# First attention half issued ahead of the convolution, and the second half's stacked queries and keys in a pool of their own

## The chip, the cores and the metric

The kernel runs on one core of a Trainium2 chip. The metric is the device time of one execution in microseconds (us); lower is better. The core has a tensor engine (PE) for matmuls and transposes, a vector engine (DVE), a scalar engine (ACT), a general engine (POOL), and a sync engine (SP) that here only issues transfers (DMAs). Each engine works through a queue of its own, strictly in order; an instruction that waits for another engine or for a transfer holds up all that stands behind it in its queue.

## The reference: what is computed

One layer of a decoder with D = 1024, for 1024 prompt tokens and 8 samples of 8 new tokens (T = 1088 rows together):

```
h    = rmsnorm(x);  proj = h @ w_in
o_rw = RWKV-7 time mixing(proj)             # 4 heads of 64
o_cv = cb * conv3(cc * cx)                  # short causal convolution, 256 channels
o_sb = stick_breaking(q, k, v)              # 8 heads of 64
x    = x + concat(o_rw, o_cv, o_sb) @ w_out
x    = x + square(relu(rmsnorm(x) @ w_up)) @ w_down
x    = x + sigmoid(rmsnorm(x) @ w_ple_gate) * (p @ w_ple_proj)
```

Stick-breaking attention, for a query at position i and keys j < i: z = q.k/8 + bias, and the weight of key j is sigmoid(z_j) times the product of (1 - sigmoid(z_m)) over all m with j < m < i. That product is a running product over the keys, taken from the last key backwards. The new sample tokens also attend to 512 cached keys, which lie in pages whose row numbers come from `page_table`.

## The kernel before

**Numbers.** Every matmul of weights is computed to fp32 accuracy as three matmuls of high and low parts (hi·hi, hi·lo, lo·hi): in lines 169 to 171 for the input projection, the convolution among it, and in lines 1093 to 1095 for the output projection and the MLP. The high part of a weight is a cast on ACT (`wh`, lines 158 and 1073), the low part a subtraction, mostly on POOL (`wl`, lines 159 and 1074).

**What sets the order.** The program writes the work in an order of emission, and a scheduler then fixes each engine's queue before the run: what was emitted earlier comes first where it can, and later work is put into the gaps that the scheduler's own estimate shows. `run(*gens)` (line 654) takes generators and advances them in turn, one step of each; so `run(*[conv]*5, *[att]*4)` emits five steps of the convolution for every four of the attention. Memory comes from pools on two sides of the on-chip memory; a tile of a pool waits for those who last used the memory under it (`reuse_waits="tile"`).

**The stretch in question.** After the RWKV part comes `wkv_sample_chunk`, then the convolution together with the first half of the attention (query rows 0 to 511), then part A (rows 0 to 511) of the output projection and the MLP, and beside it the second half of the attention (query rows 512 to 1023), and later the cached pages (`decode`) and part B.

- `convolution` (line 975): 18 pieces of 24 matmuls (432 in all), each piece evicted by ACT or DVE; three loads of weights of 1024 columns, each split by ACT (L158) and POOL (L159).
- `attention(ap, q0, q1, ...)` (line 875) has 16 units, 8 heads by two blocks of 256 queries. `prep(h)` loads for a head the stacked keys and queries (`stk_k`, `stk_q`, `stk_x`) and `vs`, on SP. `weights` takes two groups of 128 queries, each with L keys (128 to 512 in the first half, 640 to 1024 in the second). For each group: scores on PE in chunks of 512 columns (L913, L914); two sigmoids on ACT, `beta` (L915) and `keep` (L916); the mask on the last 128 columns on POOL, for `keep` and for `beta` (L920); the running product on DVE (L922); and `beta * keep` (L924) on DVE, for every other group of the second half on POOL. `values`, two units later, transposes the weights on PE (L942), splits them in `wth` (ACT) and `wtl` (DVE, L61), and multiplies with `vs` (L952, L953); ACT and DVE evict `o` (L955, L956), and SP stores it.
- Part A: `load_x` transposes the rows of x on PE (L1302). `load_mix` loads the mixed rows (`mixl`) and splits them in `mh` (ACT, L1289) and `ml` (DVE, L1290). `out_proj(A, 0, 4)` multiplies by the first half of `w_out` in 96 matmuls of 512 columns, 24 for each DVE eviction pair (L1395).
- `page_rows` loads the page table (`pti`) and computes row numbers `idx` on DVE (L1113, L1114); `row_constants` makes masks for the samples (POOL and DVE, L1131 to L1170); then POOL issues four fetches of cached pages with these row numbers (`kpg`, L1118).

The names `b`, `b_6783` and so on in rows are buffers of the accumulators (banks).

Of the kernel before, what the change touches and what calls it, by code (L numbers as in the profile page):

```python
# [21 lines left out]
F32 = mybir.dt.float32  # L22
F32R = mybir.dt.float32r
# [20 lines left out]
CA = (5, 4)  # L44
AB_ = 2
# [3 lines left out]
def hybrid_step(ctx: ExitStack, tc: tile.TileContext, I, O):  # L49
# [6 lines left out]
    def f(t):  # L56
        return t.bitcast(F32)
# [9 lines left out]
    def banks(*ids):  # L67

        turn = itertools.cycle(ids)

        def take():
            i = next(turn)
            return psum.tile([128, 512], F32, name=f"b{i}", bufs=1)

        return take
# [28 lines left out]
    km = tc.alloc_tile_pool(name="wkv_masks", bufs=1, side="right", reuse_waits="tile")  # L104
# [549 lines left out]
    def run(*gens):  # L654

        gens = list(gens)
        while gens:
            for g in list(gens):
                if next(g, gens) is gens:
                    gens.remove(g)  # L660
# [103 lines left out]
    kp = tc.alloc_tile_pool(name="wkv", bufs=1, side="right", reuse_waits="tile")  # L764
    wkv_prompt_chunks()
    kp.release()
    kp = tc.alloc_tile_pool(name="wkv_s", bufs=1, side="right", reuse_waits="tile")
    ap = tc.alloc_tile_pool(name="att_a", bufs=1, side="right", reuse_waits="tile")
# [103 lines left out]

    def attention(ap, q0, q1, zbank, wbank, obank, AHEAD):

        bias = ap.tile([128, 2, 8], F32, name="bias")
        src = I["sb_bias"]
        SP.dma_start(bias[:, 0], bass.AP(tensor=src.tensor, offset=src.offset, ap=[[0, 128], [1, 8]]))
        V.tensor_scalar(bias[:, 1], bias[:, 0], -1.0, None, op0=ALU.mult)  # L880
# [3 lines left out]
        def prep(h):  # L884

            stk = []
            for name, n, r0 in (("k", 1, 0), ("q", 0, 256 * q0), ("x", 0, 256 * q0)):
                r = slice(r0, 256 * q1)
                o = ap.tile([128, 256 * q1 - r0], F32R, name=f"stk_{name}", bufs=2)
                if name == "x":  # L890
                    for e in range(2):
                        SP.dma_start(f(o)[64 * e:64 * e + 64], stk_s[n, h, 1 - e, :, r])
                else:
                    SP.dma_start(f(o), stk_s[n, h, :, :, r].rearrange("e d t -> (e d) t"))
                stk.append(o)
            vs = ap.tile([128, 2 * q1, 128], F32R, name="vs", bufs=2)
            SP.dma_start(f(vs), v_s[h, 0:2 * q1].rearrange("i p e -> p i e"))
            heads[h] = stk + [vs]
# [59 lines left out]

        units = [(h, qb) for h in range(8) for qb in range(q0, q1)]
        prep(0)  # L960
        for n in range(len(units) + AHEAD):
            if n < len(units):
# [72 lines left out]

    wkv_sample_chunk(banks(2))
    conv, att = convolution(), attention(ap, 0, 2, banks(3, 4), banks(5, 6), banks(7), AA)
    run(*[conv] * CA[0], *[att] * CA[1])
    cv.release()
    wpool.release()  # L1040
    hpool.release()
# [435 lines left out]
    w_out = I["w_out"][0]  # L1477

    A = Part(xpa, wka, hpa, 0, 512, ((0, 512),))
    A.load_x(acc)  # L1480
    A.load_mix(range(0, 4))
    out_proj(A, 0, 4)
    A.load_mix(range(4, 8))
    ap.release()
    kp.release()
    km.release()
    pre = tc.alloc_tile_pool(name="pages", bufs=1, side="right", reuse_waits="tile")
    page = page_rows(pre)
    db, neg, own, same = row_constants(pre)
    first = [page(pre, "kpg", krows, 0, n, 4) for n in range(PAGES)]  # L1490
    ap = tc.alloc_tile_pool(name="att_b", bufs=1, side="right", reuse_waits="tile")
    run(attention(ap, 2, 4, banks(3, 4), banks(5, 6), banks(7), AB_))
    ap.release()
    dp = tc.alloc_tile_pool(name="dec", bufs=1, side="right", reuse_waits="tile")
    decode()
    dp.release()
# [5 lines left out]
    B.load_x(tr)  # L1502
    out_proj(A, 4, 4)
    A.norm("g_mlp", acc, wide=True)
    u = up(A, 0)
# [111 lines left out]
```

## Time and profile before

| | |
|---|---|
| time of three runs, us | 1713.23, 1717.89, 1720.93; median 1717.89 |
| the profiled execution, us | 1714.63, with a span of 1712.9 |
| PE busy | 1645.4 us, 96% of the span; mean granted clock 0.983 |
| DVE, ACT, POOL busy | 1082.4, 792.7 and 704.4 us (63%, 46%, 41%) |
| chain of work that ended last | PE 79%, DVE 8%, DMA 5%, ACT 3% |

The profile gives the profiled execution alone; its time is 3.3 us below the median of the three runs. The granted clock is the share of TensorE's full clock that the chip allowed: 1.00 is 2.4 GHz, and a row at half of it is 1.2 GHz. In rows of a timeline the first number is the start in us from the start of the span, the second the busy time in us, and a bracket at the end gives the idle time ahead of the row on its engine and what ended it. A pitch is the distance between the starts of two rows.

### The profile page before, as it was taken

To read this page: it belongs to the slowest core of one execution; us is meant where nothing else is said; L and a number is where in the kernel's file an instruction comes from. 1 tells how busy PE (TensorE), PEld (TensorE's weight loads), DVE (VectorE), ACT (ScalarE), POOL (GpSimd) and SP (SyncE) were. 2 spreads that over 40 slices of the span, in tenths; PEclk is the share of its full clock that TensorE was granted. 3 is DMA by queue.
4 is the path that set the end of the run, shared out by engine and by line. 5 is a ranking of instruction groups with operands and counts; after the bars stand their busy time and mean duration, and the time that the engine had idled before them with its cause. 6 is when DMAs were issued, how large, how long until landed. Compare 5 with 4: busy or idle time off the path is not lost.

```text
span 1712.9 us, 30744 instructions
## 1 busy us (share of the span) xinstructions
PE 1645.4 (96%) x11901; PEld 1485.0 (87%) x11901; DVE 1082.4 (63%) x1830; ACT 792.7 (46%) x1563; POOL 704.4 (41%) x754
## 2 busy tenths in 40 slices
PE   6999999999899899999999999998899999999998
PEld 5898988889888777888887778977899999999898
DVE  6266844465276859878753345267877888778432
ACT  6633433333353657666544444463443444438321
POOL 4123221123332654443435544365755556538210
PEclk9999999999999899999999999999999999999999
DMA  6134466235523763443345556221322232222211
GB/s 189 52 116 132 144 165 170 69 89 152 154 76 115 217 180 104 129 127 102 91 132 172 166 160 210 90 74 50 111 88 86 90 96 87 87 84 77 82 46 41
DMA packets 207061, 197.03 MB, mean 115 GB/s; under 512 B 58113, under 2 KB 172449, under 8 KB 206786
## 3 DMA queue, kind: packets, MB, share of 16 engines
q1 hardware_dynamic: 197186, 174.08, 34.2%
q0 software_dynamic: 5120, 16.78, 3.3%
q10 hardware_dynamic: 4608, 4.20, 1.0%
q8 instruction: 94, 1.54, 0.4%
q14 instruction: 53, 0.43, 0.1%
HBM read 158.03 MB, written 36.98 MB: 114 GB/s over the span
## 4 chain that ended last, share of the span: by engine, by line
PE 79%; DVE 8%; DMA 5%; ACT 3%; issue 2%; SPq 1%; POOL 1%; ACTq 0%; POOLq 0%; DVEq 0%
PE b L1093 14%; PE b L1095 14%; PE b L1094 13%; PE b L1438 3%; PE b L1437 3%; PE b L1436 3%; PE b L169 3%; PE b L170 3%; PE b L171 3%; PE b L797 2%; PE b L795 2%; PE b L942 2%; PE b L796 2%; DVE keep L922 1%; DMA wr<-in_w_in 1%
## 5 line engine op out<-in xcount | busy, mean ns | idle before, releaser
L1074 POOL TENSOR_TENSOR wl<-wr,wh 128x512 fp32r<-128x512 f32 x172 | 237.9, 1393 | 249.2 <-ACT wh L1073 232.6
L1073 ACT CAST wh<-wr 128x512 fp32r<-128x512 f32 x292 | 179.3, 622 | 293.4 <-PE b L1094 207.0
L1093 PE MATMUL b<-ah,wh 128*128 128x288 f32 (+1 forms) x768 | 255.6, 333 | 6.4 <-DVE x L1475 3.5
L1475 DVE TENSOR_TENSOR x<-b,x 128x288 f32<-128x288 f32 (+1 forms) x384 | 199.1, 527 | 98.7 <-PE b L1095 97.5
L1094 PE MATMUL b<-al,wh 128*128 128x288 f32 (+1 forms) x768 | 252.5, 329 | 0.0
L1095 PE MATMUL b<-ah,wl 128*128 128x288 f32 (+1 forms) x768 | 252.3, 329 | 0.0
L1093 PE MATMUL b<-nh,wh 128*128 128x512 f32 (+1 forms) x448 | 165.8, 371 | 1.0 <-DVE x L1395 1.0
L1094 PE MATMUL b<-nl,wh 128*128 128x512 f32 (+1 forms) x448 | 164.9, 368 | 0.8 <-DVE nl L1317 0.8
L1095 PE MATMUL b<-nh,wl 128*128 128x512 f32 (+1 forms) x448 | 165.0, 368 | 0.0
L1093 PEld LDWEIGHTS b<-ah,wh 128*128 128x128 f32 x768 | 144.9, 189 | 18.7 <-DVE x L1475 6.1
L1095 PEld LDWEIGHTS b<-ah,wl 128*128 128x128 f32 x768 | 144.8, 189 | 10.4
L1094 PEld LDWEIGHTS b<-al,wh 128*128 128x128 f32 x768 | 144.9, 189 | 9.5 <-issue 0.8
L795 PE MATMUL b<-wh,h_hi 128*128 128x256 f32 x432 | 127.0, 294 | 5.1 <-ACT sq L805 5.1
L797 PE MATMUL b<-wh,h_lo 128*128 128x256 f32 x432 | 126.5, 293 | 0.0
L796 PE MATMUL b<-wl,h_hi 128*128 128x256 f32 x432 | 124.5, 288 | 0.0
L169 PE MATMUL b<-h_hi,wh 128*128 128x384 f32 (+1 forms) x336 | 114.3, 340 | 1.9 <-ACT xs L333 1.3
L159 POOL TENSOR_TENSOR wl<-wr,wh 128x1024 fp32r<-128x1024 f32 x26 | 64.8, 2507 | 121.4 <-ACT wh L158 121.3
L170 PE MATMUL b<-h_lo,wh 128*128 128x384 f32 (+1 forms) x336 | 113.2, 337 | 0.3 <-DVE h_lo L201 0.3
L171 PE MATMUL b<-h_hi,wl 128*128 128x384 f32 (+1 forms) x336 | 111.8, 333 | 0.0
L922 DVE TENSOR_TENSOR_SCAN keep<-keep,onesq 128x128 f32<-128x128 f32 (+3 forms) x64 | 97.6, 1525 | 21.1 <-POOL keep L920 17.9
L1074 DVE TENSOR_TENSOR wl<-wr,wh 128x512 fp32r<-128x512 f32 x120 | 100.2, 837 | 9.6 <-ACT wh L1073 7.9
L1074 POOL TENSOR_TENSOR wsl<-s,wsh 128x512 fp32r<-128x512 f32 x64 | 88.5, 1404 | 37.9 <-ACT wsh L1073 37.8
(425 smaller groups left out, 4312.9 us busy)
## 6 DMA issues: line engine op xcount, KB each, us to landing
wr<-in_w_up SPq DMA_DIRECT2D x64, 512.0 KB
wr<-in_w_down SPq DMA_DIRECT2D x64, 512.0 KB
wr<-in_w_in SPq DMA_DIRECT2D x26, 512.0 KB
wr<-in_w_out SPq DMA_DIRECT2D x16, 512.0 KB
xt<-in_x_prompt SPq DMA_DIRECT2D x8, 512.0 KB
stk_s<-sth ACTq DMA_DIRECT2D x32, 128.0 KB
stk_s<-stl SPq DMA_DIRECT2D x32, 128.0 KB
v_s<-spl SPq DMA_DIRECT2D x16, 256.0 KB
```

What stands on the lines that cost most here:

```text
L169: PE.matmul(ps[:, :n], wh[:, k, c], a, start=(k == 0), stop=False)
L170: PE.matmul(ps[:, :n], wh[:, k, c], b, start=False, stop=False)
L171: PE.matmul(ps[:, :n], wl[:, k, c], a, start=False, stop=(k == nk - 1))
L795: PE.matmul(o, a, w[0][:, k, :], start=(k == 0), stop=False)
L796: PE.matmul(o, a, w[1][:, k, :], start=False, stop=False)
L797: last = PE.matmul(o, b, w[0][:, k, :], start=False, stop=(k == 7))
L1073: S.copy(h3, src)
L1074: (sub or G).tensor_sub(l3, src, f(h3))
L1093: PE.matmul(ps[:, :n], w(0, k, m), a, start=(k == 0), stop=False)
L1094: PE.matmul(ps[:, :n], w(0, k, m), b, start=False, stop=False)
L1095: PE.matmul(ps[:, :n], w(1, k, m), a, start=False, stop=(k == nk - 1))
L1475: V.tensor_add(p.x[:, m, t0:t0 + n], ps[:, :n], p.x[:, m, t0:t0 + n])
```

## The change

The first half of the attention is now emitted whole, and the convolution after it. The second half's generator is made before part A's loads, and its first step (`next(steps)`) is taken there: it emits the bias, the loads of heads 0 and 1, and the scores and weights of the first unit. The rest of it (`run(steps)`) stands where the whole stood. Its `bias` and `stk_*` tiles are in a pool of their own (`stk_b`), and the pools of the earlier parts on that side are released ahead of part A's loads, for this and for the pool of the pages.

```diff
-    def attention(ap, q0, q1, zbank, wbank, obank, AHEAD):
-
-        bias = ap.tile([128, 2, 8], F32, name="bias")
+    def attention(ap, q0, q1, zbank, wbank, obank, AHEAD, sp=None):
+
+        sp = sp or ap
+        bias = sp.tile([128, 2, 8], F32, name="bias")
...
-                o = ap.tile([128, 256 * q1 - r0], F32R, name=f"stk_{name}", bufs=2)
+                o = sp.tile([128, 256 * q1 - r0], F32R, name=f"stk_{name}", bufs=2)
...
     conv, att = convolution(), attention(ap, 0, 2, banks(3, 4), banks(5, 6), banks(7), AA)
-    run(*[conv] * CA[0], *[att] * CA[1])
+    run(att)
+    run(conv)
...
     A = Part(xpa, wka, hpa, 0, 512, ((0, 512),))
+    ap.release()
+    kp.release()
+    km.release()
+    pre = tc.alloc_tile_pool(name="pages", bufs=1, side="right", reuse_waits="tile")
+
+    sp = tc.alloc_tile_pool(name="stk_b", bufs=1, side="right", reuse_waits="tile")
+    ap = tc.alloc_tile_pool(name="att_b", bufs=1, side="right", reuse_waits="tile")
+    steps = attention(ap, 2, 4, banks(3, 4), banks(5, 6), banks(7), AB_, sp)
+    next(steps)
     A.load_x(acc)
     A.load_mix(range(0, 4))
     out_proj(A, 0, 4)
     A.load_mix(range(4, 8))
-    ap.release()
-    kp.release()
-    km.release()
-    pre = tc.alloc_tile_pool(name="pages", bufs=1, side="right", reuse_waits="tile")
     page = page_rows(pre)
     db, neg, own, same = row_constants(pre)
     first = [page(pre, "kpg", krows, 0, n, 4) for n in range(PAGES)]
-    ap = tc.alloc_tile_pool(name="att_b", bufs=1, side="right", reuse_waits="tile")
-    run(attention(ap, 2, 4, banks(3, 4), banks(5, 6), banks(7), AB_))
+    run(steps)
     ap.release()
+    sp.release()
```

Line numbers of the changed program are one higher from line 877 on, two higher from line 1040 on.

Three places of the scheduled queues follow, as text, without times.

PE where the attention's first scores stand. Before, 120 of the convolution's 432 matmuls stand ahead of the first score (L913); `L512` is a matmul of the RWKV sample chunk:

```order
L171 MATMUL b_5459<-h_hi_81,wl 128x384
L913 MATMUL b_5509<-stk_k,stk_q 128x128
L914 MATMUL b_5509<-stk_k,stk_x 128x128
L913 MATMUL b_5523<-stk_k,stk_q 128x256
L914 MATMUL b_5523<-stk_k,stk_x 128x256
L169 MATMUL b_5678<-h_hi_80,wh 128x320
```

Of the change, where 11 matmuls of the convolution stand ahead of it:

```order
L170 MATMUL b_6285<-h_lo_82,wh 128x384
L914 MATMUL b_5365<-stk_k,stk_q 128x128
L914 MATMUL b_5379<-stk_k,stk_q 128x256
L171 MATMUL b_6285<-h_hi_80,wl 128x384
L169 MATMUL b_6285<-h_hi_81,wh 128x384
L170 MATMUL b_6285<-h_lo_83,wh 128x384
L171 MATMUL b_6285<-h_hi_81,wl 128x384
L915 MATMUL b_5365<-stk_k,stk_x 128x128
```

The scores moved forward by about a hundred of the convolution's matmuls, and the convolution goes on behind them.

PE from the convolution's last matmul on. Before, the first half's scores (of 128 and 256 keys) and values are still under way there:

```order
L171 MATMUL b_6509<-h_hi_81,wl 128x320
L913 MATMUL b_6550<-stk_k,stk_q 128x128
L914 MATMUL b_6550<-stk_k,stk_x 128x128
L757 MATMUL b_5320<-ident,GS 64x64 x16
L952 MATMUL b_6423<-wth,vs 128x256
L953 MATMUL b_6423<-wtl,vs 128x256
```

Of the change: the first half is over (54 of the convolution's matmuls stand behind its last value), and the second half's scores follow, then the transposes of its first weights (L943):

```order
L171 MATMUL b_6783<-h_hi_81,wl 128x320
L914 MATMUL b_6864<-stk_k,stk_q 128x512
L914 MATMUL b_6869<-stk_k,stk_q 128x128
L915 MATMUL b_6864<-stk_k,stk_x 128x512
L915 MATMUL b_6869<-stk_k,stk_x 128x128
L914 MATMUL b_6883<-stk_k,stk_q 128x512
L915 MATMUL b_6883<-stk_k,stk_x 128x512
L914 MATMUL b_6888<-stk_k,stk_q 128x256
L915 MATMUL b_6888<-stk_k,stk_x 128x256
L914 MATMUL b_7227<-stk_k,stk_q 128x512
L915 MATMUL b_7227<-stk_k,stk_x 128x512
```

From there to the output projection's first matmul the change has 15 chunks of scores, 19 transposes of weights, 10 matmuls of values and 32 transposes of x; the projection now waits behind transposes of the second half's weights, where before it waited behind the end of the first half.

POOL at the page fetches. Before, they stand behind the first half's last masks (`beta` and `keep`, L920), and 14 splits of weights follow ahead of the second half's first mask:

```order
L920 AFFINE_SELECT beta<-beta 128x128
L1074 TENSOR_TENSOR wl<-wr,wh 128x512 x2
L920 AFFINE_SELECT keep<-keep 128x128
L1118 DMA kpg<-in_cache_k,idx 128x512 x4
L1074 TENSOR_TENSOR wl<-wr,wh 128x512 x11
L909 MEMSET keep 128x1 x3
L1074 TENSOR_TENSOR wl<-wr,wh 128x512 x3
L920 AFFINE_SELECT beta<-beta 128x128
```

Of the change:

```order
L1158 MEMSET neg 128x256
L1120 DMA kpg<-in_cache_k,idx 128x512 x4
L1076 TENSOR_TENSOR wl<-wr,wh 128x512 x2
L910 MEMSET keep 128x1 x3
L921 AFFINE_SELECT beta<-beta 128x128
L921 AFFINE_SELECT keep<-keep 128x128
L1076 TENSOR_TENSOR wl<-wr,wh 128x512 x2
L921 AFFINE_SELECT beta<-beta 128x128
L921 AFFINE_SELECT keep<-keep 128x128
```

The four fetches now stand directly ahead of the second half's first masks, with only two splits between. On DVE the row numbers `idx`, for which the fetches wait, stand behind the convolution's last evictions, in both versions, and in the changed one the second half's first running products, ahead of which they stand, follow:

```order
L1028 TENSOR_TENSOR cc<-b_6783,cc 128x256
L1031 TENSOR_TENSOR ue<-b_6783,cc 128x64
L1115 TENSOR_SCALAR idx<-pti 128x32
L1170 TENSOR_TENSOR biases<-biases 128x8
L1116 ISA idx<-idx,io 128x64
L1171 TENSOR_REDUCE db<-biases 128x1
L1172 TENSOR_SCALAR db<-db 128x1
L923 SCALAR_TENSOR_TENSOR keep<-keep,onesq 128x640
L925 TENSOR_TENSOR beta<-beta,keep 128x640
L923 SCALAR_TENSOR_TENSOR keep<-keep,onesq 128x768
L923 SCALAR_TENSOR_TENSOR keep<-keep,onesq 128x896
```

Between the eviction and the running product stand only these small operations.

## Rows read from the trace of the kernel before

**Rows 1.** The page: busy time of each engine over the span (share, instructions).

```profile
PE 1645.4 (96%) x11901; PEld 1485.0 (87%) x11901; DVE 1082.4 (63%) x1830; ACT 792.7 (46%) x1563; POOL 704.4 (41%) x754
```

**Rows 2.** Busy time by stretch: start and end in us, their difference, then the busy time of PE, PEld (weight loads), DVE, ACT and POOL with their instructions, the mean granted clock, the share of the DMA engines and what they moved in GB/s.

```profile
456.00:480.00 24.00, 20.54 (x127) 19.25 (x126) 13.16 (x21) 12.39 (x28) 11.70 (x23) 0.86 0.19 58
480.00:556.00 76.00, 75.93 (x623) 66.04 (x622) 55.92 (x109) 35.84 (x82) 20.13 (x57) 1.00 0.34 103
556.00:580.00 24.00, 16.07 (x81) 13.79 (x79) 22.13 (x62) 20.30 (x46) 15.64 (x31) 0.73 0.84 260
...
612.00:670.00 58.00, 51.58 (x234) 42.03 (x234) 46.97 (x49) 42.47 (x81) 32.01 (x37) 0.94 0.46 134
```

**Rows 3.** The waits of PE from 430 to 670 us: who waits for whom, us in total, times, the longest.

```profile
PE b L942 <- DVE wtl L61: 5.5, 3, 2.8
PE b L942 <- DVE beta L924: 3.5, 1, 3.5
PE b L953 <- DVE qm_i L1135: 2.4, 1, 2.4
PE b L952 <- DVE o L956: 2.2, 1, 2.2
```

**Rows 4.** PE's timeline at the convolution's first matmul, and after the one long wait beside the convolution.

```profile
428.87 0.34 PE L169 MATMUL b<-h_hi,wh 128*128 128x384 f32 x1
...
466.27 0.48 PE L942 MATMUL b<-ident,beta 128*128 128x128 f32 x1 [3.46 <-DVE beta L924]
...
470.70 0.52 PE L170 MATMUL b<-h_lo,wh 128*128 128x384 f32 x1
...
471.31 0.34 PE L169 MATMUL b<-h_hi,wh 128*128 128x384 f32 x1
```

**Rows 5.** SP's timeline, where the first half's first loads are issued, and where the second half's are.

```profile
427.89 0.43 SPq L894 DMA_DIRECT2D stk_q<-stk_s  x1
...
607.46 0.43 SPq L894 DMA_DIRECT2D stk_q<-stk_s  x1
```

**Rows 6.** PE's timeline at the convolution's last matmul, at the projection's first, and at the second half's first score.

```profile
552.29 0.31 PE L171 MATMUL b<-h_hi,wl 128*128 128x320 f32 x1
...
578.77 0.78 PE L1093 MATMUL b<-mh,wh 128*128 128x512 f32 x1
...
613.51 0.56 PE L913 MATMUL b<-stk_k,stk_q 128*128 128x512 f32 x2 [1.41 <-DMA stk_q<-stk_s]
...
614.63 0.87 PE L914 MATMUL b<-stk_k,stk_x 128*128 128x512 f32 x2 [0.28 <-DMA stk_x<-stk_s]
...
617.54 0.62 PE L1095 MATMUL b<-mh,wl 128*128 128x512 f32 x1
...
618.23 0.40 PE L1094 MATMUL b<-ml,wh 128*128 128x512 f32 x1
```

**Rows 7.** POOL's timeline at the page fetches, and at the second half's first mask.

```profile
578.38 2.05 POOL L1118 DMA_INDIRECT kpg<-in_cache_k,idx  x1 [0.18 <-DVE db L1170]
...
584.28 0.95 POOL L1118 DMA_INDIRECT kpg<-in_cache_k,idx  x1 [0.30 <-issue]
585.25 5.02 POOL L1074 TENSOR_TENSOR wl<-wr,wh 128x512 fp32r<-128x512 f32 x4
592.06 2.54 POOL L1074 TENSOR_TENSOR wl<-wr,wh 128x512 fp32r<-128x512 f32 x2 [1.78 <-ACT wh L1073]
...
617.03 0.29 POOL L920 TENSOR_SCALAR_AFFINE_SELECT beta<-beta 128x128 f32<-128x128 f32 x1 [1.86 <-ACT beta L915]
```

**Rows 8.** DVE's timeline: the convolution's last eviction, the row numbers, two splits of mixed rows, and the second half's first running product.

```profile
552.98 0.21 DVE L1030 TENSOR_TENSOR ue<-b,cc 128x64 f32<-128x64 f32 x1
...
576.40 0.34 DVE L1113 TENSOR_SCALAR idx<-pti 128x32 int32<-128x32 int32 x1
...
576.77 1.23 DVE L1114 CUSTOM_DVE_ANT_0 idx<-idx,io 128x64 uint16<-128x64 uint16 x1
...
580.62 1.27 DVE L1290 TENSOR_TENSOR ml<-mixl,mh 128x512 fp32r<-128x512 f32 x2
...
584.63 6.20 DVE L1290 TENSOR_TENSOR ml<-mixl,mh 128x512 fp32r<-128x512 f32 x1 [0.23 <-ACT mh L1289]
...
617.61 1.49 DVE L922 TENSOR_TENSOR_SCAN keep<-keep,onesq 128x640 f32<-128x640 f32 x1
```

**Rows 9.** Groups of instructions by line and shape from 430 to 900 us: count, busy us, mean ns of one, and the idle time ahead of them with what ended it.

```profile
L922 DVE TENSOR_TENSOR_SCAN keep<-keep,onesq 128x1024 f32<-128x1024 f32 x8 | 21.0, 2631 | 0.0
L922 DVE TENSOR_TENSOR_SCAN keep<-keep,onesq 128x896 f32<-128x896 f32 x8 | 18.3, 2286 | 0.9 <-POOL keep L920 0.9
L922 DVE TENSOR_TENSOR_SCAN keep<-keep,onesq 128x768 f32<-128x768 f32 x8 | 15.1, 1886 | 2.1 <-POOL keep L920 2.0
L922 DVE TENSOR_TENSOR_SCAN keep<-keep,onesq 128x640 f32<-128x640 f32 x8 | 14.9, 1860 | 3.9 <-POOL keep L909 2.7 <-POOL keep L920 1.3
L924 DVE TENSOR_TENSOR beta<-beta,keep 128x896 f32<-128x896 f32 x8 | 8.6, 1081 | 0.0
L924 DVE TENSOR_TENSOR beta<-beta,keep 128x640 f32<-128x640 f32 x8 | 7.8, 977 | 0.0
L61 DVE TENSOR_TENSOR wtl<-b,wth 128x512 fp32r<-128x512 f32 x48 | 32.2, 679 | 11.5 <-ACT wth L60 9.8 <-PE b L942 1.4
L1290 DVE TENSOR_TENSOR ml<-mixl,mh 128x512 fp32r<-128x512 f32 x8 | 10.9, 1376 | 0.3 <-ACT mh L1289 0.2
```

## The prediction

> **What bounds the kernel now.** The page comes first: PE is busy for 96% of the span [rows 1], so the kernel is bound by PE's work, and a reordering that leaves this work as it is can only move the 67 us in which PE does nothing and the time in which its clock is at half. The second view is the table of stretches [rows 2]. From 480 to 556 us, where the convolution and the first half of the attention run side by side, PE has 75.93 of 76 us busy at clock 1.00: nothing is to be had there. It loses in three places that the change touches: 456 to 480 (20.54 of 24 busy, clock 0.86), 556 to 580 (16.07 of 24, clock 0.73) and 612 to 670 (51.58 of 58). The third view, the waits [rows 3], tells on whom: not on transfers for the most part but on DVE, which is late with `beta`, `wtl`, the constants `qm_i` and `o`. The fourth is PE's timeline. A wait there costs more than itself: after the wait of 3.46 us the convolution's matmuls last 0.52 us instead of 0.34 until about 471.0 [rows 4], that is 4.75 us at half clock, 2.4 of them lost. The projection's matmuls after the waits at 613.5 do the same (0.62 against 0.40) for some 4 us, 1.9 lost [rows 6].
>
> I take the place between the convolution's last matmul (552.29) and the projection's first (578.77) as the measure of the change: a gap of 26.5 us [rows 6]. Of it 7.7 us are waits (5.5 + 2.4 + 2.2 from [rows 3], less the 2.8 that lies later, and a wait of 0.4). The clock of 0.73 over 16.07 us of work means another 4.3 lost [rows 2]. So 14.5 us are work, 12.0 lost.
>
> **What the change does, part by part.** No matmul, cast or byte is added. Everything is order.
>
> *First half ahead of the convolution.* The first score stands behind 11 of the convolution's matmuls instead of 120, so PE reaches it at about 428.87 + 11 × 0.174 = 430.8 [rows 4] (0.174 us is the pitch that 0.34 us matmuls have in 462 to 473). Its `stk_q` is issued at 427.89. The second half's `stk_q`, issued at 607.46 [rows 5], had PE waiting until 613.51 [rows 6]: 6.05 us. By that it lands at 433.9, and PE waits for 3.1 us, with the half clock behind it, where before it worked. Against this the wait of 3.46 us may go. It came of a DVE product that was itself held up, and the same operations meet in the new order. Neither bound has a nearer row: at best the wait and its slow clock are gone and the loads come in time, a gain of 3.46 + 2.4 = 5.9; at worst the wait stays and the other comes on top, a loss of 3.1 + 2.4 = 5.5. I take 0, halfway, since the two have the same size.
>
> *The gap behind the convolution.* In the new order the first half is over by then; 54 of the convolution's matmuls cover its end, and the constants `qm_i` run under this cover too, so the waits of 5.5, 2.4 and 2.2 us in their present form go. The work in the gap, counted in the new queue (15 score chunks, 19 + 32 transposes, 10 matmuls of values), is about as much as before, 14.5 us. But the projection's first matmul now stands behind the transposes of the second half's weights, and these come out of a chain over POOL and DVE that begins only when the convolution ends. From the last matmul's start:
>
> - The last eviction ends at 552.98 + 0.21, 0.9 us after it. `idx` follows (0.34, a small one, then 1.23 [rows 8]): **2.6**.
> - POOL issues the four fetches, which waited for `idx`: 578.38 to 585.25 [rows 7], 6.9 us: **9.5**. Before, this held up nothing but splits of weights. Now the masks stand behind it.
> - Two `wl` (2.54) and two masks (0.29 each) [rows 7]: **12.6**.
> - DVE, means of [rows 9]: the running product of 640 keys 1.86, product 0.98; POOL's two next `wl` and masks end together with that, at about **15.6**. Then 768 keys 1.89, 896 keys 2.29, product 1.08, 1024 keys 2.63: **23.5**.
> - Two `ml` and two `wtl` of 512 columns, 0.64 [rows 8] and 0.68 each: 2.6. The next 640 keys 1.86, two more `ml` 1.3, product 0.98, `wtl` 0.42 (half a `wtl` of 512 and some): **30.7**.
> - PE's transposes, chunks and values behind it, ahead of the projection: some 1.7, by the count of the queue: **32.5**.
>
> The sums of [rows 9] have `ml` at 1.376 on the mean, which is one piece of 6.20 us [rows 8] among pieces of 0.64; with that mean for four of them the chain is 35.3. I take the middle, **34**. The low bound takes each stage by its shortest row: the fetches at 0.95 each with 0.3 between (4.7, not 6.9), 1.49 instead of 1.86 for the 640 keys and the others in that proportion (2.1 less): 28. The high bound is a rival, below. So the gap is 34 instead of 26.5: **+7.5**.
>
> *The clock behind the gap.* Before, the projection's first matmuls ran slow for some 1.4 us; after waits as long as the new ones the half clock lasted for 4.0 to 4.75 us [rows 4, 6]. I put down **+1.5**.
>
> *The second half's loads.* They are issued behind the first half's last reads, well ahead of the first score, so the wait of 1.41 + 0.28 us at 613.5 with its 1.9 of slow clock goes [rows 6]: **−3.5** (bounds: −3.6, and 0 if the second half's later loads wait in their place; the transfers of 556 to 580 already take 0.84 of the DMA engines [rows 2]). The releases and pools themselves cost no instruction. SP's second load of `w_out`, `xr` and `mixl` now stand behind the convolution's last stores, some 2 us after the convolution; they are needed at the end of the chain above, which covers them, and it would cost the time by which they come later than 30 us. The memory that the pool `stk_b` takes moves waits of the pages and of `att_b`, which I cost at nothing for the same reason.
>
> *Later.* From the decode on the queue of PE reads the same in both. 0.
>
> The sum: 0 + 7.5 + 1.5 − 3.5 = +5.5. Against the profiled execution, 1714.63 + 5.5 = **1720**. That execution lies 3.3 us below the median of 1717.89, so against the median this is 2 us, and I count it as no change: about 0.5% (8.6 us) is what a measurement of this kernel can tell, so 1709.3 and 1726.5 are the limits.
>
> **A rule against the change.** The 6.20 us of `ml` began at 584.63, and POOL was in four `wl` from 585.25 for 5.02 us; `ml` ended 0.5 us after them, where two others took 1.27 together while POOL only issued fetches [rows 7, 8]. The Trainium skill, "SBUF — State Buffer", section "Who interferes with whom", says that a VectorE operation with two inputs in SBUF and a GpSimd operation that reads SBUF use one port pair under an exclusive lock, and the later one blocks for the other's whole length. The trace's 6.20 us agrees that the two exclude each other, not on who yields: by the recorded starts POOL came second and DVE waited. Were the rule at work at each such meeting in the new gap, the time would be that of the first rival below, 1728, against 1720 by the mean rows.
>
> **The rivals.**
>
> *Slower, by POOL and DVE holding each other up in the gap (24%).* If every DVE operation of the chain with two inputs in memory waits for POOL's split or product beside it, as `ml` did, the chain grows by what POOL does meanwhile: two `wl` beside the 640 keys (2.54), a POOL product of 768 beside the 896 keys (1.6 by the proportion of the `wl`, 1.27 for 512 columns), and four `wl` beside the second `ml` pair (5.02) [rows 7]: 32.5 + 9.2 = 41.7, that is +15.2 + 1.5 − 3.5 = +13.2, **1728**. For it: the row of 6.20. Against it: the means of [rows 9] already hold ordinary collisions. It decides from a gap of 37 to 38 us upward; from 40.4 the kernel is slower by over 0.5%.
>
> *Slower, by a denser first half (8%).* DVE has 55.92 of 76 us busy in 480 to 556 [rows 2]. The same attention work packed before the last 54 convolution matmuls raises this by about a tenth. One more wait like that of 3.46 with its 2.4 of slow clock adds 5.9, to 1726; two make **1732**.
>
> *Faster (18%).* The gap at its low bound, 28 us: +1.5 + 1.5 − 3.5 = −0.5; and the first half at its best, −5.9: **1708**. For it: the fetches that took 0.95 us each, and 75.93 of 76 us busy, which shows that the convolution can fill every wait of the attention. Against it: `stk_q` issued only 2.9 us before it is wanted.
>
> *Nothing is moved on the whole (12%).* The waits change places and their sum stays: **1715**. For it: the work in the gap is the same, 14.5 us, and DVE was the one waited for before and is again.
>
> **How the numbers follow.** The forecast (38%), 1720, has 1715 to 1726 as its own range. The range of 1706 to 1732 takes in the faster case and the two slower ones but for their ends. Faster by over 0.5%: 0.18, the faster case. Slower: 0.30, the two slower rivals less 2 in a hundred, which fall short. Same: the rest, 0.52.
>
> **What would show it.** In the changed kernel's trace: POOL's fetches start 2 to 3 us after the convolution's last matmul (if 6 or more, the page table is late), the first mask of the second half comes about 9 us after them, PE's waits in the gap are on `beta` and `wtl` and come to 18 us or more, and the gap is 30 to 37 us. PE waits for `stk_q` at about 431. No wait for `stk_q` remains in the second half, and the clock over the gap lies below 0.73. The prediction is wrong if the gap is under 28 (fetches or masks not on the path) or over 40 (DVE held up), or if the stretch of the convolution loses more than 6 us where it lost almost none.

## The result and the profile after

The changed kernel takes 1723.46 us (median of 10 runs, 1719.39 to 1725.46) against 1718.62 us of the kernel before (10 runs): a ratio of 1.0027 with a 95% interval of 1.0015 to 1.0039, that is 2.6 to 6.7 us slower; the two medians lie 4.8 us apart. The forecast was 1720, which is 5.5 us above the profiled execution and 2 above the median of three known then. By the bound of 0.5% this is no change, as forecast. The profiled execution took 1724.79 us, 10.2 more than the one of before; so the pair of profiles shows about twice the difference that the medians show, and what of that is chance is told below.

The page, busy time of each engine; the work is that of [rows 1]:

```profile
PE 1649.2 (96%) x11901; PEld 1485.8 (86%) x11901; DVE 1079.2 (63%) x1830; ACT 792.3 (46%) x1563; POOL 709.7 (41%) x754
```

Busy time by stretch of the changed kernel, columns as in [rows 2]:

```profile
456.00:480.00 24.00, 24.00 (x170) 22.55 (x170) 19.39 (x30) 18.34 (x44) 17.02 (x31) 1.00 0.54 164
480.00:556.00 76.00, 74.83 (x608) 64.51 (x608) 57.08 (x113) 35.83 (x83) 20.11 (x58) 0.98 0.22 60
556.00:580.00 24.00, 13.08 (x65) 11.12 (x63) 5.84 (x40) 7.39 (x16) 7.64 (x12) 0.79 0.87 240
580.00:612.00 32.00, 22.77 (x116) 19.70 (x117) 27.63 (x22) 25.32 (x51) 21.89 (x29) 0.79 0.76 244
612.00:670.00 58.00, 56.05 (x278) 46.27 (x277) 45.10 (x53) 33.30 (x67) 39.37 (x39) 1.00 0.42 124
```

Beside the convolution PE now loses nearly nothing in 456 to 480, where it lost 3.46 us and its clock [rows 2]; from 612 to 670 it loses 2 us where it lost 6.4. All this and more is lost in one hole between 556 and 612, where PE does nothing for 20.2 us. From 556 to 580 DVE, ACT and POOL are busy for 5.84, 7.39 and 7.64 of 24 us, where before they had 22.13, 20.30 and 15.64: the three mostly stand, while the DMA engines are at 0.87. Whom PE waits for from 425 to 680 us (who for whom, us in total, times, the longest):

```profile
PE b L914 <- ACT keep L917: 8.2, 2, 7.1
PE b L943 <- DVE beta L925: 5.4, 1, 5.4
PE b L954 <- DVE wtl L61: 3.7, 1, 3.7
PE b L914 <- DMA stk_q<-stk_s: 2.4, 2, 1.9
PE b L915 <- DMA stk_x<-stk_s: 1.8, 2, 1.4
PE b L953 <- DVE o L957: 1.3, 1, 1.3
```

PE's timeline from the convolution's last matmul to the projection's first, the rows with long waits:

```profile
564.20 0.31 PE L171 MATMUL b<-h_hi,wl 128*128 128x320 f32 x1
...
566.88 0.53 PE L915 MATMUL b<-stk_k,stk_x 128*128 128x512 f32 x2 [1.36 <-DMA stk_x<-stk_s]
574.50 0.80 PE L914 MATMUL b<-stk_k,stk_q 128*128 128x512 f32 x1 [7.09 <-ACT keep L917]
...
584.43 0.69 PE L943 MATMUL b<-ident,beta 128*128 128x128 f32 x2 [5.36 <-DVE beta L925]
...
597.32 0.58 PE L954 MATMUL b<-wtl,vs 128*128 128x256 f32 x1 [3.71 <-DVE wtl L61]
...
604.46 0.40 PE L1095 MATMUL b<-mh,wh 128*128 128x512 f32 x1
```

The gap is 40.3 us, against 26.5 before [rows 6], with 20.2 us of waits against 7.7 and a granted clock of 0.70 against 0.77. The longest wait, 7.1 us for ACT, is not the one that the projection hangs on: behind it PE waits for DVE's `beta` until 584.43 all the same. What stands behind these waits is told by four queues. SP issues the page table's load and w_out's first load only when the convolution is over, directly behind the second half's loads of heads 0 and 1, which begin at 559.13:

```profile
563.49 1.09 SPq L893 DMA_DIRECT2D stk_x<-stk_s  x2
564.62 0.58 SPq L1112 DMA_DIRECT2D pti<-in_page_table  x1
...
566.25 0.38 SPq L1069 DMA_DIRECT2D wr<-in_w_out  x1
```

In the kernel before, w_out's first two loads went out ahead of the convolution's last matmul (552.29):

```profile
550.87 0.94 SPq L1067 DMA_DIRECT2D wr<-in_w_out  x2
```

ACT stands in front of a cast of that w_out for 16 us, the last 8 of them behind the convolution's last matmul, with the second half's sigmoids behind it:

```profile
572.15 1.14 ACT L1075 CAST wh<-wr 128x512 fp32r<-128x512 f32 x2 [16.03 <-DMA wr<-in_w_out]
573.19 0.68 ACT L916 ACTIVATE beta<-b,bias 128x512 f32<-128x512 f32 x1
```

On DVE the row numbers wait for the page table, and the running products for POOL:

```profile
570.57 0.18 DVE L1115 TENSOR_SCALAR idx<-pti 128x32 int32<-128x32 int32 x1 [5.46 <-DMA pti<-in_page_table]
...
579.50 4.02 DVE L923 TENSOR_TENSOR_SCAN keep<-keep,onesq 128x640 f32<-128x640 f32 x1 [8.09 <-POOL keep L921]
...
586.41 3.37 DVE L923 TENSOR_TENSOR_SCAN keep<-keep,onesq 128x896 f32<-128x896 f32 x1 [0.37 <-POOL keep L921]
...
593.60 3.07 DVE L1292 TENSOR_TENSOR ml<-mixl,mh 128x512 fp32r<-128x512 f32 x2
```

POOL issues the four fetches, splits w_out, and only then masks; its later products stand beside the long operations on DVE:

```profile
571.42 1.18 POOL L1120 DMA_INDIRECT kpg<-in_cache_k,idx  x1 [27.59 <-DVE db L1172]
...
575.41 0.95 POOL L1120 DMA_INDIRECT kpg<-in_cache_k,idx  x1 [0.30 <-issue]
576.38 2.50 POOL L1076 TENSOR_TENSOR wl<-wr,wh 128x512 fp32r<-128x512 f32 x2
...
578.93 0.28 POOL L921 TENSOR_SCALAR_AFFINE_SELECT beta<-beta 128x128 f32<-128x128 f32 x1
579.18 0.28 POOL L921 TENSOR_SCALAR_AFFINE_SELECT keep<-keep 128x128 f32<-128x128 f32 x1
579.45 2.48 POOL L1076 TENSOR_TENSOR wl<-wr,wh 128x512 fp32r<-128x512 f32 x2
...
586.36 1.54 POOL L925 TENSOR_TENSOR beta<-beta,keep 128x768 f32<-128x768 f32 x1
...
593.77 2.35 POOL L925 TENSOR_TENSOR beta<-beta,keep 128x1024 f32<-128x1024 f32 x1 [2.41 <-DVE keep L923]
```

So the first mask comes 14.7 us after the convolution's last matmul.

### The profile page after: what moved, and what is told of

It reads as the page before. It is cut to its first block, busy times and chain, and to the rows that moved or that the text cites. A ratio compares the mean times of both kernels' runs of the same rounds, so it can differ in the third digit from the quotient of the medians.

```text
span 1723.0 us, 30802 instructions
## 1 busy us (share of the span) xinstructions
PE 1649.2 (96%) x11901; PEld 1485.8 (86%) x11901; DVE 1079.2 (63%) x1830; ACT 792.3 (46%) x1563; POOL 709.7 (41%) x754
## 4 chain that ended last, share of the span: by engine, by line
PE 76%; DVE 9%; DMA 4%; issue 3%; ACT 3%; POOL 2%; SPq 1%; ACTq 0%; POOLq 0%; DVEq 0%
PE b L1095 13%; PE b L1097 13%; PE b L1096 13%; PE b L1440 3%; PE b L1439 3%; PE b L1438 3%; PE b L169 3%; PE b L170 3%; PE b L171 2%; PE b L797 2%; PE b L795 2%; PE b L796 2%; PE b L943 1%; DMA wr<-in_w_in 1%; DVE keep L923 1%
## 5 line engine op out<-in xcount | busy, mean ns | idle before, releaser
L1097 PEld LDWEIGHTS b<-ah,wl 128*128 128x128 f32 x768 | 145.2, 189 | 10.4
```

Source lines behind the costliest of these rows:

```text
L1097: PE.matmul(ps[:, :n], w(1, k, m), a, start=False, stop=(k == nk - 1))
```

## The experiments

Each ratio below is to executions of the kernel before in the same session. Their median lay between 1714.9 and 1720.5 us, while the expectations name times against 1718.6; so a range in us is best read as a difference from that.

**Both kernels once more, for a second profile.**

> The changed kernel once more, for a second profile. If the ledger of the first profile is a matter of the kernel, the gap is 39 to 42 us again with 19 to 21 us of waits, and the stretch from the convolution's first to its last matmul 132 to 135 us. If single executions move it, the gap or the stretch differs by 3 us or more.

> The kernel before once more, for a second profile. If the ledger is a matter of the kernel, the stretch of the convolution is 122 to 125 us and the gap 25.5 to 27.5 us with 7 to 8.5 us of waits; the start of the convolution, which lay 2 to 5 us earlier in the first profile than in those of the other kernels although the program is the same up to there, tells how far single executions differ: 430 us or later if the first profile was a fast one.

PE's timeline of the changed kernel, second profile:

```profile
565.14 0.31 PE L171 MATMUL b<-h_hi,wl 128*128 128x320 f32 x1
...
605.03 0.40 PE L1095 MATMUL b<-mh,wh 128*128 128x512 f32 x1
```

And of the kernel before:

```profile
556.13 0.31 PE L171 MATMUL b<-h_hi,wl 128*128 128x320 f32 x1
...
582.83 0.77 PE L1093 MATMUL b<-mh,wh 128*128 128x512 f32 x1
```

The gaps are 39.9 and 26.7 us, within 0.4 of the first profiles, and the stretch from the convolution's first to its last matmul is 133.1 (133.1 in the first) and 122.3 (123.4). Gap and stretch belong to the kernels. What moves is the part ahead: the convolution's first matmul is at 428.87 and 433.88 in two executions of the kernel before, and at 431.14 and 432.01 in the changed one, though the queue up to there is the same. From that matmul to the end the four profiles take 1284.1 and 1287.4 against 1291.8 and 1291.9 us, that is +6.1 on the mean. Of the 10 us between the first two profiles 7.7 lie there and 2.3 ahead of it.

**Each half of the change alone.**

```diff
 # first half alone: the kernel before with
-    run(*[conv] * CA[0], *[att] * CA[1])
+    run(att)
+    run(conv)
 # second half alone: the changed kernel with this undone
```

> Only the first half of the attention is emitted ahead of the convolution; the second half stands where it stood before, in its old pool. Theory A (the second half's early start makes the gap: its weights' chain stands ahead of the projection): nothing holds the projection but its own loads, the gap between the convolution's last matmul and the projection's first is under 25 us, the time is 1712 to 1718 us (before: 1718.6). Theory B (the gap comes of having nothing left to do when the convolution ends, since transfers for what follows are issued only then): the gap's waits stay 15 us or more, on transfers of w_out and of mixl, and the time is 1720 to 1726.

> Only the second half's part of the change: its pool, the earlier releases and the first step ahead of part A's loads; convolution and first half are interleaved 5 to 4 as before. Theory A: the projection again waits for the second half's first weights, the time is 1721 to 1727 us. Theory B: the rest of the first half covers the transfers as before, the gap loses 12 us or less and the wait at the second half's first score goes; 1712 to 1717.

The first half alone: 1.0015 (0.9998 to 1.0033). PE's timeline and SP's at the convolution's end (last matmul at 566.04):

```profile
577.13 1.09 PE L1303 MATMUL b<-ident,xr 128*128 128x128 f32 x4 [10.78 <-DMA xr<-in_x_prompt]
...
584.63 3.08 PE L1303 MATMUL b<-ident,xr 128*128 128x128 f32 x12 [3.42 <-DMA xr<-in_x_prompt]
587.36 0.78 PE L1094 MATMUL b<-mh,wh 128*128 128x512 f32 x1
```

```profile
571.58 0.38 SPq L1068 DMA_DIRECT2D wr<-in_w_out  x1
572.05 2.02 SPq L1300 DMA_DIRECT2D xr<-in_x_prompt  x4
```

The gap is 21.3 us, under 25 as theory A had it. But two thirds of it are waits, and the time, 1722.93 us against 1720.47, lies in B's range, though the interval takes in no change: with no attention left to do, PE waits 14.4 us, not for w_out or the mixed rows as B had it, but for x, whose loads stand on SP behind stores and a third load of w_out. The second half alone: 1.0021 (1.0005 to 1.0037). Its gap is 27.5 us with 6.6 of waits, as in the kernel before, so theory A is wrong on the wait: the rest of the first half hides the second half's chain. But it is not faster, as B had it; it is 3.0 us slower by the medians, in A's range. PE's waits from 428 to 680 show one reason:

```profile
PE b L1094 <- DVE x L1396: 6.9, 3, 3.6
```

The projection's evictions now stand on DVE among the second half's running products. Thus each part alone costs little, with a different gap, and the hole of the changed kernel comes of both: the first part takes the cover away, and the second puts a chain of 40 us where the cover was. That the time of the changed kernel comes of this hole is not shown by it: 1.0015 and 1.0021 for gaps of 21.3 and 27.5 us stand beside 1.0027 for 40.3.

**The page fetches out of the masks' way, in two ways.**

```diff
 # late: behind the sixth unit of the second half (late: its weights)
...
+    V.tensor_scalar(zero, late[:, 0:32], 0.0, None, op0=ALU.mult)
+    V.tensor_add(page.idx, page.idx, zero)
 # early: four columns of row numbers, ahead of run(att)
+    SP.dma_start(idx0, ...page_table...)
+    V.tensor_scalar(idx0, idx0, 128, None, op0=ALU.mult)
+    V.tensor_add(idx0, idx0, io0)
...
```

> The changed kernel, but the four page fetches wait for a row number that is made to depend on the weights of the second half's sixth unit (a zero computed from them is added), so POOL issues them some 70 us later, behind the first masks. Theory of the prediction (POOL's fetches are on the path): the first mask comes 5 us earlier or more than at 14.7 us after the convolution's last matmul, the gap is 35 us or less, the time 1716 to 1719. Rival (the scalar engine, held by the late load of w_out until 8 us after the convolution, sets the first mask): the mask comes at most 4 us earlier, the gap is 36 to 40 us, the time 1719.5 to 1723.

> The changed kernel, but the row numbers of the first four page fetches are computed ahead of the convolution (the page table's load of these too), so the fetches need not wait for the page table behind the convolution. Theory of the prediction: the fetches are over when the convolution ends or 5 us after it, the first mask comes 5 us earlier or more, the gap is 35 us or less, the time 1716 to 1719. Rival (scalar engine held by w_out): the mask comes at most 4 us earlier, 1719.5 to 1723.

> The kernel with early row numbers once more. If early row numbers give back what the change cost, its gap is 27 to 30 us again and its ratio to the kernel before 0.998 to 1.002. If the first ratio was a matter of the executions, it comes out at 1.003 to 1.006, as for the variant in which the queue ahead of the convolution stayed as it was.

Late (the fetches go at 666.03): the mask comes 10.7 us after the convolution, 4.0 earlier, as the rival had it, and the gap falls to 33.2, as the prediction's theory had it. But the time does not fall: 1.0033 (1.0017 to 1.0049), which neither expected. Early: mask at 8.0, gap 28.2, ratio 1.0005 (0.9989 to 1.0020); again, gap 28.1, ratio 0.9997 (0.9983 to 1.0010). That is level with the kernel before, and the second is clear of the changed one. The rows of the first (last matmul at 569.17) show POOL and ACT:

```profile
572.21 4.95 POOL L1083 TENSOR_TENSOR wl<-wr,wh 128x512 fp32r<-128x512 f32 x4 [25.52 <-ACT wh L1082]
577.20 0.31 POOL L921 TENSOR_SCALAR_AFFINE_SELECT beta<-beta 128x128 f32<-128x128 f32 x1
```

```profile
571.50 1.14 ACT L1082 CAST wh<-wr 128x512 fp32r<-128x512 f32 x2 [7.64 <-DMA wr<-in_w_out]
573.09 1.14 ACT L1082 CAST wh<-wr 128x512 fp32r<-128x512 f32 x2 [0.45 <-DMA wr<-in_w_out]
574.13 0.68 ACT L916 ACTIVATE beta<-b,bias 128x512 f32<-128x512 f32 x1
```

The edit had a side effect: w_out's first two loads are issued 1.4 us ahead of the last matmul, not 2 and 5 behind it, so ACT's first cast comes 2.3 us after it instead of 8. And PE's queue is another one well ahead of the gap: in the two traces at least 370 of the 3783 matmuls ahead of the convolution stand in another order, and as many of the 1005 from its first matmul to its last. The convolution begins at 434.29 and 436.00 us, 2 to 5 later than in the changed kernel's profiles. So these two runs change more than the fetches. A further run took this away.

**Early row numbers, with the rest of the queue as in the changed kernel.**

```diff
+    late = [next(att) for _ in range(4)][-1]
...
+    V.tensor_scalar(idx0, late[:, 0:4], 0.0, None, op0=ALU.mult)   # then the load, as above
```

> As the kernel with early row numbers, but these are made to depend on the first half's fourth unit (a zero computed from its weights is written ahead of the page table's load), so that nothing moves ahead of the attention: PE's queue is that of the changed kernel up to the convolution's last matmul. In the earlier kernels with early row numbers the queue ahead of the convolution had moved, and the convolution began 2 to 6 us later. Theory (the fetches behind a late page table cost what the gap shows, and the shifted start ate it): gap 27 to 30 us, the convolution's start at 429 to 434 us, the time 3 to 7 us under the changed kernel, which is level with the kernel before or up to 3 us under it. Rival (what the gap gives is lost elsewhere whatever the start): within 2 us of the changed kernel, 4 us over the one before.

PE's order is that of the changed kernel up to the convolution's last matmul (563.47). The fetches stand 20 us ahead of it, but ACT's first cast is late again, and with it the mask (ACT's row, then POOL's):

```profile
570.77 1.14 ACT L1084 CAST wh<-wr 128x512 fp32r<-128x512 f32 x2 [15.37 <-DMA wr<-in_w_out]
```

```profile
574.02 0.31 POOL L921 TENSOR_SCALAR_AFFINE_SELECT beta<-beta 128x128 f32<-128x128 f32 x1
```

Mask 10.5, gap 33.4, just as with late fetches: the theory's 27 to 30 us are not reached. The ratio is 1.0058 (1.0042 to 1.0075), some 10 us over the kernel before, slower than either side expected; the rival's thought, that what the gap gives is lost elsewhere, is the nearer one. In both runs the gap stops at 33 us, with the cast of w_out on ACT next ahead of the mask. The fetches alone are not what the time hangs on.

**w_out out of the sigmoids' way, in two ways.**

```diff
 # first two loads of w_out cast and split on DVE (with early row numbers)
+    *((V, V.tensor_copy) if p is A and k0 == 0 and m0 == 0 else ())
 # or held: their buffer is first written from the second half's first weights
+    V.tensor_scalar(raw[:, 0:1], hold.pop()[:, 0:1], 0.0, None, op0=ALU.mult)
```

> The kernel with early row numbers (the run before this one), and the first two loads of w_out cast and split on DVE, so that neither ACT's sigmoids nor POOL's masks of the second half stand behind this transfer. Theory (the late w_out, through ACT and POOL, is what is left of the delay of the second half's first weights): the first mask comes 3 to 4 us after the convolution's last matmul instead of 8, the gap falls from 28 to 22 to 25 us, the time lies 3 to 6 us under that kernel and 2 to 5 under the kernel before. Rival (the loads of x and of the mixed rows, issued on SP behind the convolution's last stores, end last anyway): waits on xr of 3 us or more stand in the gap, it stays at 26 us or more, and the time is within 2 us of that kernel.

> Early row numbers, and the first two loads of w_out made to wait for the first weights of the second half (a column of their buffer is first written from them), so that the casts of w_out stand behind the first sigmoids on ACT, and its splits behind the first masks on POOL. Theory (two things hold the second half's first weights: POOL in the page fetches, ACT and POOL in a w_out that has not landed): the first mask comes 3 to 5 us after the convolution's last matmul, the waits in the gap fall to 6 to 9 us, the gap to 21 to 26, the time to 3 to 7 us under the changed kernel and 0 to 4 under the kernel before. Rival (the chain over DVE and the loads of x take the place): the mask is early, but the gap stays at 27 us or more, and the time is no better than with early row numbers alone.

> The changed kernel with w_out held as in the run before, the row numbers late as in the changed kernel. Theory (both hold it): POOL's fetches still stand ahead, the first mask comes 11 to 13 us after the convolution's last matmul instead of 14.7, the gap is 33 to 38 us, the time within 3 us of the changed kernel. If the late w_out alone were the cause, the mask would come at 4 to 6 us and the gap fall under 30.

> The run before with the first two loads of w_out held behind the second half's first weights. Theory: gap 24 to 27 us; but the loads held back come later, so the time is within 2 us of the run before. If holding w_out alone is a gain, 2 to 4 us under it; if the held loads are missed later, 2 to 5 us over it, with waits of PE beyond the gap of 9 us or more (6 in the changed kernel).

On DVE: the mask comes at 2.4 us, but the casts and splits of w_out now stand on DVE ahead of the first running product, which starts 7.1 us after the last matmul (567.63), and ACT waits for the next load of w_out (ACT's row, then DVE's):

```profile
576.67 1.14 ACT L1082 CAST wh<-wr 128x512 fp32r<-128x512 f32 x2 [6.45 <-DMA wr<-in_w_out]
```

```profile
573.57 1.28 DVE L1083 TENSOR_TENSOR wl<-wr,wh 128x512 fp32r<-128x512 f32 x2
574.77 1.48 DVE L923 TENSOR_TENSOR_SCAN keep<-keep,onesq 128x640 f32<-128x640 f32 x1
```

The gap is 29.1 and the ratio 1.0058 (1.0039 to 1.0077), slower than either side expected. Held, with early row numbers: mask at 2.4, gap 25.9, both as the theory had it, but with 11.0 us of waits, not 6 to 9, since PE now waits for x:

```profile
583.90 1.97 PE L1315 MATMUL b<-ident,xr 128*128 128x128 f32 x8 [5.82 <-DMA xr<-in_x_prompt]
```

1.0026 (1.0012 to 1.0040): in the time the rival is right, no better than early row numbers alone. Held, with late row numbers: mask at 10.7 behind the fetches, about as expected, gap 36.0, and 1.0067 (1.0054 to 1.0079), slower than expected. Held on top of the dependent row numbers: mask at 3.8, gap 27.4, 1.0039 (1.0023 to 1.0055), by the medians 3.3 us under the run without the hold; the two intervals overlap. So the hold went with a loss twice and with a gain once.

Taken together, from the timelines (waits of PE over 0.15 us; "later" is from the projection's first matmul to 900 us). The waits come from one execution each, the ratio from all of a kernel; the profiled one with late fetches was the slowest of its 12 (1730.2 us, median 1726.73), that with dependent rows the fastest of its 6 (1720.59, median 1726.89):

| kernel | first mask | gap | waits in it | later | sum | ratio |
|---|---|---|---|---|---|---|
| before (two profiles) | | 26.5, 26.7 | 7.7, 7.8 | 6.7, 6.6 | 14.4, 14.4 | 1 |
| early row numbers (two) | 8.0, 8.3 | 28.2, 28.1 | 10.8, 11.7 | 5.9, 4.4 | 16.6, 16.1 | 1.0005, 0.9997 |
| second half alone | | 27.5 | 6.6 | 12.4 | 19.0 | 1.0021 |
| early rows, w_out held | 2.4 | 25.9 | 11.0 | 9.0 | 20.1 | 1.0026 |
| early rows, split on DVE | 2.4 | 29.1 | 12.7 | 9.5 | 22.2 | 1.0058 |
| first half alone | | 21.3 | 14.4 | 8.0 | 22.4 | 1.0015 |
| dependent rows, w_out held | 3.8 | 27.4 | 10.4 | 12.7 | 23.1 | 1.0039 |
| dependent rows | 10.5 | 33.4 | 15.3 | 9.0 | 24.3 | 1.0058 |
| late fetches | 10.7 | 33.2 | 15.8 | 9.6 | 25.4 | 1.0033 |
| changed (two) | 14.7, 14.1 | 40.3, 39.9 | 20.2, 20.6 | 6.0, 5.8 | 26.2, 26.3 | 1.0027 |
| w_out held | 10.7 | 36.0 | 16.9 | 9.7 | 26.6 | 1.0067 |

The gap's length alone does not order the times, and the sum of the waits does so only roughly: the two smallest sums are the fastest kernels, but the changed kernel, with nearly the largest, is not among the slowest. In most variants with a shorter gap more is waited later (9 to 13 us instead of 6). No variant beats the kernel before.

## Why the prediction was right, and where its steps were off

**The time and the side: right, the size in part by luck.** The median of 1723.46 us lies in the forecast's own range of 1715 to 1726, and the change stays within 0.5%. The +5.5 beside a measured +4.8 is a closer match than the steps deserve. It was counted from an execution of 1714.63 us, 4 us below the median of ten; and with the gap as measured, the prediction's own sum is 0 + 13.8 + 1.5 − 3.5 = +11.8, or 1726. Terms that were too small and too large made up for each other.

**The gap: right place, too small.** 40.3 and 39.9 us in the two profiles, against 34 taken and 32.5 summed. That is at the prediction's own sign of being wrong (over 40, DVE held up), and nearer to the 41.7 of its first rival than to 34. *The start:* `idx` was summed as ready at 2.6 us, behind the last eviction; it came at about 6.9, since the page table's load was issued only at 564.62 and DVE waited 5.46 us for it. The text named that sign ("if 6 or more, the page table is late") but gave it no price, and did not see that the change's own loads stand directly ahead of the page table on SP. With the first half alone, where they come later, this load goes at 559.20, 6.8 us ahead of the last matmul. The fetches took 5.0 us, not 6.9, near the low bound, so they ended at 12.2 instead of 9.5, and the first two masks at 15.3 instead of 12.6: 2.7 us of the 7.8 that the gap is over its sum. *DVE:* from the first mask on the chain was summed with means, and these were too short here: 4.02 us for the 640 keys, where the same operation takes 1.49 in the kernels with no split of POOL beside it; 3.37 for 896 keys (2.02 with early row numbers); 3.07 for two `ml` (1.27 in [rows 8]). Over the means that were summed these three are 5.0 us, nearly all of the other 5.1. *ACT:* the cast of w_out in front of the sigmoids was not in the sum at all; it held the sigmoids until 573.19. In the changed kernel POOL is later still; when the fetches are taken away, this cast is what comes next.

**The rival of POOL and DVE** came half true: it had 9.2 us for these meetings, and the three long operations are 5.7 us over their undisturbed durations. Two are those that it named. The third is not: the second pair of `ml`, for which it had 5.02 us, took 1.26, and the first pair was held, beside POOL's product of 1024 keys. 4.02 is what is left of the two splits, 579.50 to 581.93, and the 1.49 of the operation alone, with 0.10 over. That agrees with the rule of the Trainium skill ("SBUF — State Buffer", section "Who interferes with whom") that was weighed, in that the later one waits: here POOL's split had started 0.05 us earlier. But DVE waited for both splits, not for one operation, and with dependent rows, where POOL's split was 0.07 us earlier, by its length for one alone.

**The first half: 0 taken, it gained.** The waits beside the convolution fell from 6.1 us to 3.5, and with the slow clock (by the granted clock) from some 8 to some 5. The first head's `stk_q`, for which a wait at 431 was forecast, was not waited for in the first profile (0.55 us in the second): it was issued at 429.76 and its score went at 433.31, 3.55 us later and not 6.05. There were 0.48 us for `stk_x` at 434.96, and 1.91 for the next head's `stk_q`; the 3.46 went.

**The second half: the size right.** The wait for `stk_q` at 613.5 is gone; but with the score itself it moved into the gap, where PE waits 0.48 us for `stk_q` and 1.36 for `stk_x` (0.36 and 0.70 in the second profile) ahead of a longer wait. The loads go out 4.3 us ahead of that score, not well ahead. From the projection to 900 us PE waits 6.0 us, not 6.7, and the half clock costs some 2 us less there, by the granted clock of the four profiles. The forecast was −3.5, the gain about 3.

**The clock behind the gap: wrong place.** +1.5 was put down for slow matmuls of the projection. The row at 604.46 has 0.40 us, the full clock. PE worked through the end of the gap on transposes and scores, and the half clock lay inside the gap (0.70 over it, below 0.73 as the text had it), where by the granted clock it cost some 6 of PE's 20.1 us of work, against some 4 of 18.6 before.

**The sum.** Gap +13.8, first half −3, second half −3 make about +8 in the profiles, whose stretch from the convolution on is 6.1 longer on the mean; the medians say +4.8. Beyond idle time and half clock some 3 us of PE's time remain, which I put down to unlike matmuls that alternate more often; that was not tested. Behind 900 us, where the prediction had 0, the changed kernel's two profiles lose some 5 us less to idle time and half clock; whether that is the kernel's is not shown. Two profiles of one program can differ as much: with early row numbers this stretch takes 1285.1 and 1276.5 us. I cannot settle which figure is nearest.

**What stays open:** what of the changed kernel's 4.8 us comes of the gap, and why early row numbers are level with the kernel before while the variants with a gap as short or shorter are not. They differ in when w_out is issued and in PE's queue ahead of the convolution and beside it, all of which the edit moved; only these together were run.

## What to carry to other kernels

Where one stage ends and loads for the next can only then be issued, independent work behind the stage's end keeps the hole small: with it the gap stayed at 27.5 us, without it 40.3. But a shorter hole is not yet a shorter kernel; here most of the variants that closed it part of the way were no faster. When work is moved, list for every engine, and for the queue that issues transfers, what stands ahead of it in the new order and which transfer that waits for: the cast of w_out, 8 us behind the convolution, held all that ACT had behind it. Where operations of two engines were seen to hold each other up, price each new meeting rather than take a mean. And a single profile pair can show twice the difference that the medians show, so compare the same stretch in two profiles of each.

## What the runs showed of the hardware that I had not expected

A running product on DVE and a split on POOL hold each other up, as it seems by whole operations: 640 keys take 1.49 us alone, 4.02 and 3.77 beside two splits (two profiles), and 2.55 to 2.56 in the kernels with late fetches and with dependent rows, where POOL's pair of splits too took longer, 3.66 and 3.68 instead of 2.50. The rows from the kernel with dependent row numbers (DVE, then POOL):

```profile
574.60 2.55 DVE L923 TENSOR_TENSOR_SCAN keep<-keep,onesq 128x640 f32<-128x640 f32 x1 [4.83 <-POOL keep L921]
```

```profile
574.53 3.68 POOL L1085 TENSOR_TENSOR wl<-wr,wh 128x512 fp32r<-128x512 f32 x2
```

One split, the running product and the other split one behind the other would take 1.25 + 1.49 + 1.25 = 4.0 us there; the pair with the wait in it took 3.7. The same program reached the same matmul at 428.87 us in one execution and at 433.88 in another, five microseconds apart, before any of the changed work began.
